# A two-layer fp32 model on one Trainium2 core: from generators advanced on an account to list scheduling of noted instructions

## The chip, the core and the metric

The kernel runs on one core of one Trainium2 chip. The metric is the device time of one execution in microseconds; lower is better. PE is the matrix engine (TensorE), PEld its weight loads, DVE the vector engine, ACT the scalar engine, POOL the GpSimd engine, SP the engine that issues the DMAs.

## What is computed

A sequence of 256 tokens (T = 256) with model width 1024 goes through two blocks of two layers each, in fp32. Every layer is a half-weighted SwiGLU feed-forward, a mixer, and a second SwiGLU feed-forward. The mixer of the first block joins a gated delta rule with stick-breaking attention; that of the second block uses three softmax attentions. Cut to what matters here:

```python
def swiglu(h, w_in, w_out):
    gate, up = jnp.split(h @ w_in, 2, axis=-1)
    return (jax.nn.silu(gate) * up) @ w_out

def hybrid_mixer(h, w_in, conv_w, a_log, dt_bias, ...):      # block 1
    dn_qkv, dn_z, dn_b, dn_a, sb_q, sb_k, sb_v, gate_a, gate_b = split_cols(h @ w_in)
    qkv = jax.nn.silu(causal_depthwise_conv(dn_qkv, conv_w))
    ...
    o_a = gated_delta_rule_chunked(q, k, v, g, beta)         # chunks of 64, a triangular solve in each
    y_a = (rmsnorm(o_a, dn_out_norm) * jax.nn.silu(dn_z)) @ w_branch_a
    y_b = stick_breaking_attention(rmsnorm(sb_q), rmsnorm(sb_k), sb_v) @ w_branch_b
    return (jax.nn.sigmoid(gate_a) * y_a + jax.nn.sigmoid(gate_b) * y_b) @ w_out
```

## The kernel before

**Dense products.** Activations lie feature-major in SBUF as `xh` and `xl`, two fp32r tiles whose sum is the fp32 value. A weight matrix is read in raw tiles of 128x1024 (four buffers, queue of SP), and each half of one, a piece of 128x512, is turned into `hi` (an fp32r copy, on ACT or by a CAST on DVE) and `lo` (a subtraction on DVE), up to seven pieces ahead of their use, in nine buffers. A product is then three matmuls per 128x128 block of weights: hi with xh, hi with xl, lo with xh. The program calls the psum tiles of these products `dn` (four of the eight banks) and those of all other work `acc` (four, shared).

**Stages.** The order is feed-forward, mixer, feed-forward, four times. The feed-forwards are dense products with little else. A mixer of block 1 (`mix1`, L736) runs, for the head pairs p = 0 to 3, the dense products dq, dk, dv, z(p-1), sq, sk, sv and ga(p), then z(3), gb(0) to gb(3), yb(0) to yb(3) (weights `w_branch_b`), and at last ya(0) to ya(3) (`w_branch_a`) and the output. Beside them stand four jobs `delta` (the delta rule of a head pair, L941: some 25 short groups of matmuls with a copy or a vector operation behind each: d_N, d_U, d_T, d_P, d_Ns, d_dec) and four jobs `stick` (L1148: b_qk, b_z, b_ss, b_tm). A mixer of block 2 (`mix2`, L1206) has softmax jobs in that place.

**What sets the order.** Every instruction is issued the moment the program reaches it, and `Clock.account` (L285) adds it to an account of the four engines. The jobs are Python generators in three queues a, b, c. Behind each k of a dense product `between` (L638) runs one short leftover (`pending`: taps of the convolution, squares) and `tick` (L497), which advances a queue by one step if the account says that the step's inputs are there and a psum bank is free:

```python
    def tick(self):
        for q in self.bg.values():
            if q and max(self.due.get(id(q), 0.0), self.nc.bank_free("acc", 4)) <= self.nc.free["tensor"]:
                self.step(q)

    def need(self, name, steps=1000):
        while self.done[name] < steps:
            self.step(min((q for q in self.bg.values() if q), key=lambda q: self.due.get(id(q), 0.0)))
```

At five places of `mix1` the program can't go on without a job: `need(("delta", p - 3))` (L804), `need(("stick", p - 1), 3)` (L822, ahead of sq(p)), `need(("delta", 1))` (L838), `need(("stick", 3))` (L845, ahead of yb) and `drain()` (L853, ahead of ya). There all steps that are left stand in a row, with no dense matmul between them.

**Choice of engine.** `split` and `copy` (L534, L547) take ACT unless the account lets DVE end it over 0.3 or 0.4 us earlier; `add` takes DVE or POOL. `acts` loads ACT's function table when the set of functions changes; a Copy needs no set of its own. In the rows of the profile nearly all instructions carry L226, the line of the helper that issues them, so they are told apart by their tiles.

Of the kernel before, what the change touches and what calls it, by code (L numbers as in the profile page):

```python
# [21 lines left out]
CP_A = 0.4  # L22
HI_A = 0.3
# [188 lines left out]

class Engine:


    def __init__(self, clock, name, eng):
        self.clock, self.name, self.eng = clock, name, eng

    def __getattr__(self, op):
        f = getattr(self.eng, op)  # L220

        def call(*args, **kw):
            aps = [a for a in list(args) + list(kw.values()) if isinstance(a, bass.AP)]
            if aps:
                self.clock.account(self.name, op, aps, kw)
            return f(*args, **kw)  # L226

        return call


class Clock:
    def __init__(self, nc):
        self.nc = nc
        self.free = {"tensor": 0.0, "vector": 0.0, "scalar": 0.0, "gpsimd": 0.0}
        self.ready = {}
        self.used = {}
        self.avail = {}
        self.slots = {}
        self.last = self.port = 0.0
        for n in self.free:  # L240
            setattr(self, n, Engine(self, n, getattr(nc, n)))
        self.sync = nc.sync

    def slot(self, pool, tag, bufs, tile_):

        h = self.slots.setdefault((pool, tag), [])
        if len(h) >= bufs:
            self.avail[tile_.tensor.name] = self.used.get(h.pop(-bufs), 0.0)
        h.append(tile_.tensor.name)
        return tile_  # L250

    def bank_free(self, tag, bufs):
        h = self.slots.get(("psum", tag), [])
        return self.used.get(h[-bufs], 0.0) if len(h) >= bufs else 0.0

    def cost(self, eng, op, out, ins):
        n = 1
        for d in (ins[0] if op == "tensor_reduce" else out).shape[1:]:
            n *= d
        psum = any(a.tensor.name.startswith(("dn_", "acc")) for a in [out] + ins)  # L260
        ptrs = sum(1 for a in ins[1:] if len(a.shape) == 2 and a.shape[1] == 1)
        if eng == "tensor":
            one = ins[0].dtype == R or op == "transpose"
            return max(n / 2.4e3, 0.107) + 0.002 if one else max(n / 0.6e3, 4 * ins[0].shape[-1] / 2.4e3) + 0.003
        if eng == "vector":
            two = not psum and op in ("tensor_copy", "tensor_scalar", "memset")
            return 0.07 + 0.06 * ptrs + n * (0.52e-3 if two else 1.04e-3) * (8 if op == "reciprocal" else 1)
        if eng == "scalar":
            return (0.055 if psum else 0.095) + n * 0.83e-3 + 0.093 * (len(ins) - 1)
        return 0.1 + n * {"tensor_scalar": 4e-3, "tensor_copy": 3.4e-3, "memset": 0.9e-3}.get(op, 2.2e-3)  # L270

    def shared(self, eng, out, ins):

        return eng == "gpsimd" or eng == "vector" and not any(
            a.tensor.name.startswith(("dn_", "acc")) for a in [out] + ins)

    def begins(self, eng, out, ins):
        at = max([self.free[eng], self.avail.get(out.tensor.name, 0.0)] + [self.ready.get(a.tensor.name, 0.0) for a in ins])
        return max(at, self.port) if self.shared(eng, out, ins) else at

    def ends(self, eng, op, out, ins):

        return self.begins(eng, out, ins) + self.cost(eng, op, out, ins)

    def account(self, eng, op, aps, kw):  # L285
        out, ins = aps[0], aps[1:]
        end = self.ends(eng, op, out, ins)
        self.free[eng] = end
        if self.shared(eng, out, ins):
            self.port = end  # L290
        for a in aps:
            self.used[a.tensor.name] = end + 0.1
        self.ready[out.tensor.name] = end + (0.07 if eng == "tensor" else 0.13)
        if eng != "tensor":
            self.last = max(self.last, end + 0.13)


class Stream:
# [43 lines left out]
    def split(self, upto):  # L342
        while self.nsplit < min(upto, len(self.pieces)):
# [6 lines left out]
            self.net.split(self.hi[u], self.lo[u], self.raw[r][:, o:o + n])  # L350
# [9 lines left out]
class Chunk:  # L360
    def __init__(self, stream, i):
        self.stream, self.i = stream, i
        self.kt, self.n = stream.shapes[i]

    def __call__(self, k, c, n):
# [8 lines left out]
        st.split(u + 1 + PIECE_AHEAD)  # L374
# [16 lines left out]
class Net:  # L391
    def __init__(self, ctx, tc, x, wsrc, small, out, parts):
        self.tc = tc
        self.nc = nc = Clock(tc.nc)
# [9 lines left out]
        self.act_set = None  # L404
        self.small_src, self.cmat_src = small
        self.bg = {"a": [], "b": [], "c": []}
        self.done = {}
        self.pending = []
        self.due = {}
# [3 lines left out]
    def t(self, shape, tag, bufs=1, dt=F, pool=None):  # L413
        self.uid += 1
        pool = pool or self.tp or self.cp
        return self.nc.slot(pool.name, tag, bufs, pool.tile(shape, dt, tag=tag, name=f"{tag}_{self.uid}", bufs=bufs))
# [7 lines left out]
    def scope(self, name):  # L424
        self.uid += 1
        old = self.tp
        with self.tc.tile_pool(name=f"{name}{self.uid}", bufs=1) as self.tp:
            yield
        self.tp = old

    def ps(self, shape, tag, bufs):
        self.uid += 1
        return self.nc.slot("psum", tag, bufs, self.pp.tile(shape, F, tag=tag, name=f"{tag}_{self.uid}", bufs=bufs))

    def bank(self, shape):
        return self.ps(list(shape), "acc", 4)

    def dn(self, shape=(128, 2, 256)):
        return self.ps(list(shape), "dn", 4)

    def acts(self, name):
        if self.act_set != name:
            self.nc.scalar.preload_act_table_set(name)
            self.nc.free["scalar"] += 1.3
            self.act_set = name
# [33 lines left out]
    def work(self, queue, name, gen):  # L479
        self.done[name] = 0  # L480
        q = self.bg[queue]
        if not q:
            self.due[id(q)] = self.nc.free["scalar"] + 0.15
        q.append((name, gen))

    def step(self, q):

        nc = self.nc
        nc.last = 0.0
        name, gen = q[0]  # L490
        self.done[name] += 1
        if next(gen, self) is self:
            q.pop(0)
            self.done[name] = 1000
        self.due[id(q)] = nc.last

    def tick(self):  # L497

        for q in self.bg.values():
            if q and max(self.due.get(id(q), 0.0), self.nc.bank_free("acc", 4)) <= self.nc.free["tensor"]:  # L500
                self.step(q)

    def need(self, name, steps=1000):

        while self.done[name] < steps:
            self.step(min((q for q in self.bg.values() if q), key=lambda q: self.due.get(id(q), 0.0)))

    def drain(self):
        for q in list(self.bg.values()):
            for name, _ in list(q):  # L510
                self.need(name)

# [3 lines left out]
    def load_x(self):  # L516
# [15 lines left out]
        self.x_sqs()  # L532

    def split(self, hi, lo, x, gain=None):  # L534

        nc = self.nc
        if gain is None:
            if nc.ends("scalar", "activation", hi, [x]) <= nc.ends("vector", "tensor_copy", hi, [x]) + HI_A:
                nc.scalar.activation(hi, x, AF.Copy)
            else:  # L540
                nc.vector.tensor_copy(hi, x)
            nc.vector.tensor_sub(lo, x, hi.bitcast(F))
# [4 lines left out]
    def copy(self, out, x, scale=None):  # L547

        nc = self.nc
        ins = [x] if scale is None else [x, scale]  # L550
        op = "tensor_copy" if scale is None else "tensor_scalar"
        if nc.ends("scalar", "activation", out, ins) <= nc.ends("vector", op, out, ins) + CP_A:
            if scale is None:
                nc.scalar.activation(out, x, AF.Copy)
            else:
                nc.scalar.activation(out, x, AF.Copy, scale=scale)
        elif scale is None:
            nc.vector.tensor_copy(out, x)
        else:
            nc.vector.tensor_scalar(out, x, scale, None, op0=OP.mult)  # L560
# [10 lines left out]
    def x_sqs(self):  # L571
        self.pending += [lambda b=b: self.x_sq(b) for b in range(4)]
# [10 lines left out]
    def add(self, out, a, b):  # L583

        nc = self.nc
        first = min(("vector", "gpsimd"), key=lambda e: nc.ends(e, "tensor_add", out, [a, b]))
        getattr(nc, first).tensor_add(out, a, b)
# [30 lines left out]
    def mm3(self, ps, w, x, js, start, stop):  # L618

        mm = self.nc.tensor.matmul  # L620
        for p, (a, b) in enumerate(((0, 0), (0, 1), (1, 0))):
            for j in js:
                mm(ps(j), w[j][a], x[b], start=(start(j) and p == 0), stop=(stop and p == 2), skip_group_check=True)
# [14 lines left out]
    def between(self, k, mid):  # L638
        if self.pending:
            self.pending.pop(0)()  # L640
        if mid and k == mid[0]:
            mid[1]()
        self.tick()

    def flush(self):
        while self.pending:
            self.pending.pop(0)()

    def dense_tok(self, key, xs, mid=None):
# [8 lines left out]
        for k in range(ch.kt):  # L658
            w = ch(k, 0, ch.n)
            for p, (a, b) in enumerate(((0, 0), (1, 0), (0, 1))):  # L660
                for i in range(2):
                    nc.tensor.matmul(ps[i], xs[a][k][:, i * 128:(i + 1) * 128], w[b],
                                     start=(k == 0 and p == 0 and (i == 0 or ch.n > 256)),
                                     stop=(k == ch.kt - 1 and p == 2), skip_group_check=True)
# [6 lines left out]
    def ffn(self, part, nxt):  # L671
# [4 lines left out]
        def out(c):  # L676
# [13 lines left out]
            final = nxt[1] == "final"  # L690
            for b in range(4):
# [12 lines left out]
            if not final:  # L704
                self.x_lo(3, g)
                self.x_sqs()

        for c in range(11):
# [880 lines left out]
```

## Time and profile before

| | us |
|---|---|
| time, median of 3 runs | 2794.15 (2793.99 to 2794.7) |
| profiled execution, its own time | 2791.08 |
| span of that execution | 2789.3 |
| PE busy | 2687.7 |
| DVE busy | 2051.2 |
| ACT busy | 1438.2 |

The profiled execution is 1.78 us longer than its span, and 3.07 us shorter than the median. The stages can be told in the trace by their tiles: the mixers of block 1 lie at 194.17 to 584.47 us and 951.31 to 1340.92 us, those of block 2 at 1708.03 to 1968.84 us and 2335.60 to 2594.08 us, the feed-forwards around them. The page has 40 slices with PE's busy share and the granted clock; the views by windows, by waits, and in order of time show each stage apart.

### The profile page before, as it was taken

What the parts mean: (1) busy time and instruction counts of PE and PEld (TensorE: products, weight loads), DVE (VectorE), ACT (ScalarE), POOL (GpSimd) and SP (SyncE); (2) the same over time, 40 slices, a digit from 0 to 9 for tenths busy, and PEclk for the clock granted to TensorE, in tenths of its full rate; (3) what the DMA queues carried; (4) which work ended last, traced back from release to release, by engine and by line L of the source; (5) the groups of instructions that cost most, each with busy time, mean ns of one, the idle gap of its engine ahead of it and who ended that gap; (6) DMA issues with size and microseconds to landing.
All of it is one profiled execution on the core that took longest, in us unless ns stands there. A gap on an engine that the chain in (4) does not pass through costs nothing.

```text
span 2789.3 us, 57423 instructions
## 1 busy us (share of the span) xinstructions
PE 2687.7 (96%) x22692; PEld 2644.8 (95%) x22692; DVE 2051.2 (74%) x4163; ACT 1438.2 (52%) x2870; POOL 75.7 (3%) x106
## 2 busy tenths in 40 slices
PE   8999799899999997998999999999999999999998
PEld 8999798899999997988999999989999999989998
DVE  7668878676676788886767767767767767767766
ACT  5456556454454575554545445545545445545543
POOL 0000001100000001010000000000000000000000
PEclk9999899999999998999999999999999999999999
DMA  6554334355555542333555554435555554445553
GB/s 232 189 177 158 122 103 148 103 186 192 195 189 190 171 170 99 111 135 118 191 195 193 196 196 148 151 135 174 193 195 175 197 196 146 157 131 182 191 188 129
DMA packets 128142, 463.45 MB, mean 166 GB/s; under 512 B 14336, under 2 KB 14592, under 8 KB 127744
## 3 DMA queue, kind: packets, MB, share of 16 engines
q1 hardware_dynamic: 127872, 459.78, 48.9%
q8 instruction: 178, 2.92, 0.4%
q14 instruction: 92, 0.75, 0.1%
HBM read 458.67 MB, written 1.05 MB: 165 GB/s over the span
## 4 chain that ended last, share of the span: by engine, by line
PE 86%; DVE 8%; ACT 3%; issue 2%; DMA 1%; DVEq 0%; SPq 0%; POOL 0%; ACTq 0%
PE dn L226 62%; PE acc L226 24%; DVE lo L226 3%; DMA raw<-in_w_dram 1%; ACT hi L226 1%; DVE d_prod L226 0%; DVE d_rows L226 0%; DVE dq L226 0%; ACT b_tm L226 0%; DVE d_dec L226 0%; DVE dk L226 0%; DVE d_Ub L226 0%; DVE pad L226 0%; DVE b_qk L226 0%; DVE d_Nb L226 0%
## 5 line engine op out<-in xcount | busy, mean ns | idle before, releaser
L226 DVE TENSOR_TENSOR lo<-raw,hi 128x512 fp32r<-128x512 f32 x1752 | 1148.9, 692 | 225.7 <-ACT hi L226 208.0
L226 ACT ACTIVATE hi<-raw 128x512 fp32r<-128x512 f32 (+1 forms) x1639 | 933.6, 617 | 265.6 <-PE dn L226 165.2
L226 PE MATMUL dn<-xh,hi 128*128 128x256 f32 x4208 | 842.6, 281 | 6.2 <-DVE hi L226 6.0
L226 PE MATMUL dn<-xl,hi 128*128 128x256 f32 x4208 | 828.2, 278 | 4.1 <-DVE xl L226 4.1
L226 PE MATMUL dn<-xh,lo 128*128 128x256 f32 x4208 | 826.7, 278 | 0.0
L226 PEld LDWEIGHTS dn<-xh,hi 128*128 128x128 f32 x4208 | 640.4, 189 | 16.3 <-issue 9.1
L226 PEld LDWEIGHTS dn<-xl,hi 128*128 128x128 f32 x4208 | 639.6, 189 | 5.8 <-DVE xl L226 5.6
L226 PEld LDWEIGHTS dn<-xh,lo 128*128 128x128 f32 x4208 | 639.2, 189 | 0.0
L226 PE MATMUL acc<-al,hi 128*128 128x256 f32 x1408 | 204.3, 282 | 0.0
L226 PE MATMUL acc<-ah,hi 128*128 128x256 f32 x1408 | 202.8, 281 | 0.0
L226 PE MATMUL acc<-ah,lo 128*128 128x256 f32 x1408 | 202.8, 281 | 0.0
L226 ACT ACTIVATE ah<-us 128x512 fp32r<-128x512 f32 x88 | 55.6, 632 | 283.4 <-DVE us L226 283.4
L226 PEld LDWEIGHTS acc<-ah,lo 128*128 128x128 f32 x1408 | 183.0, 189 | 0.0
L226 PEld LDWEIGHTS acc<-al,hi 128*128 128x128 f32 x1408 | 183.0, 189 | 0.0
L226 PEld LDWEIGHTS acc<-ah,hi 128*128 128x128 f32 x1408 | 181.6, 188 | 0.0
L226 ACT ACTIVATE gs<-gs 128x512 f32<-128x512 f32 x88 | 55.8, 635 | 228.3 <-DVE gs L226 228.3
L226 DVE TENSOR_TENSOR gs<-dn,nr 128x512 f32<-128x512 f32 x88 | 60.8, 691 | 104.3 <-PE dn L226 104.0
L226 DVE TENSOR_TENSOR us<-dn,nr 128x512 f32<-128x512 f32 x88 | 60.7, 690 | 102.2 <-PE dn L226 102.2
L226 PE MATMUL dn<-hi,xh 128*128 128x256 f32 (+2 forms) x640 | 134.7, 292 | 0.9 <-ACT v L226 0.9
L226 PE MATMUL dn<-lo,xh 128*128 128x256 f32 (+2 forms) x640 | 129.7, 284 | 0.0
L226 PE MATMUL dn<-hi,xl 128*128 128x256 f32 (+2 forms) x640 | 129.3, 283 | 0.0
L226 DVE TENSOR_TENSOR al<-us,ah 128x512 fp32r<-128x512 f32 x88 | 60.9, 692 | 61.4 <-ACT ah L226 61.4
(313 smaller groups left out, 2880.5 us busy)
## 6 DMA issues: line engine op xcount, KB each, us to landing
raw<-in_w_dram SPq DMA_DIRECT2D x853, 512.0 KB, 4.5
raw<-in_w_dram SPq DMA_DIRECT2D x14, 384.0 KB, 3.8
raw<-in_w_dram SPq DMA_DIRECT2D x4, 408.0 KB, 4.1
cmat<-in_cmat_dram SPq DMA_DIRECT2D x1, 1216.0 KB, 9.3
x<-in_x_dram SPq DMA_DIRECT2D x4, 256.0 KB, 5.4
out_dram<-x SPq DMA_DIRECT2D x4, 256.0 KB, 2.6
cmat<-in_cmat_dram SPq DMA_DIRECT2D x1, 648.0 KB, 8.0
raw<-in_w_dram SPq DMA_DIRECT2D x2, 272.0 KB, 3.1
```

What stands on the lines that cost most here:

```text
L226: return f(*args, **kw)
```

## The change

Nothing is issued any more when the program reaches it. `Sched.note` (L286 of the new program) records an instruction with its operands, works out from the regions that they cover which earlier ones it depends on, and puts it on a list. At the end of each scope (`heads` and `merge` of mix1, a feed-forward, the end) `flush` (L338) emits the whole list on the account of the engines: it takes the engine that can start something earliest, and on it the ready instruction of the lowest `rank`. On PE anything that is not a dense matmul goes first and the dense matmuls keep their order; on ACT and DVE it goes by the time of readiness, and the `hi` or `lo` of a weight piece by the time of its use less 5.0 or 4.0 us. Calls to `need`, `drain`, `tick`, `pending` and the `yield`s are gone. The core of the diff:

```diff
+    SLACK = {"vector": 4.0, "scalar": 5.0}
...
+    def rank(self, e, s, at, t):
+        if t.stream:
+            return (1, 0.0, t.seq)
+        if e in ("tensor", "sync"):
+            return (0, at if e == "tensor" else 0.0, t.seq)
+        key = at
+        if t.piece is not None:
+            n = self.use.get(t.piece, self.nstream + 12 * (t.piece - self.last))
+            key = max(s, self.free["tensor"]) + (n - self.done_stream) * 0.1135 - self.SLACK.get(e, 4.0)
+        if e == "scalar" and t.table is not None and t.table != self.table:
+            key += 2.0
+        return (0, key, t.seq)
```

```diff
+        for eng, (op, args, kw) in alts.items():
...
+            func = args[2] if eng == "scalar" and op == "activation" else None
+        t.table = self.want if "scalar" in alts and func not in (AF.Copy, AF.Square) else None
...
+        if e == "scalar" and t.table is not None and t.table != self.table:
+            self.nc.scalar.preload_act_table_set(t.table)
```

```diff
-        if nc.ends("scalar", "activation", out, ins) <= nc.ends("vector", op, out, ins) + CP_A:
...
+            self.nc.note({"scalar": ("activation", (out, x, AF.Copy), {}), "vector": ("tensor_copy", (out, x), {})})
...
-        st.split(u + 1 + PIECE_AHEAD)
+        st.split(min(u + 1 + PIECE_AHEAD, PIECE_BUFS + (u if self.held is None else self.held)))
```

Three more things change with it. The psum banks get fixed lanes: in mix1 two for each parity of `delta`, one for `stick` and three for the dense products (four before). `add` takes DVE alone. A copy or a `hi` that may run on either engine is noted with ACT's form first and DVE's second, and since `func` is taken from the last form, it carries the table that is wanted at that place of the program. Over the whole program the table loads go from 49 to 178 (in each mix1 from 13 to 63); DVE has 4050 instructions instead of 4013 (a few CASTs less, more copies), ACT 2624 ACTIVATEs instead of 2661; PE's matmuls, POOL's and SP's instructions keep their numbers. PE enters work other than dense products some 385 times in each mix1, instead of 260.

Two places. PE in the first mix1, before: the end of the dense product z(1) (`hi`, `lo` with `xh`, `xl` into dn_4352), the rows of delta and stick that follow, and the first of sq(2) (dn_4562):

```order
L226 MATMUL dn_4352<-hi_4268,xl_14_85 128x256 x2
L226 MATMUL dn_4352<-lo_4269,xh_9_80 128x256 x2
L226 MATMUL acc_4444<-b_z_3633,sbv_3172 128x256
L226 MATMUL acc_4444<-b_z_3633,sbv_3172 128x128
L226 MATMUL acc_4451<-d_T_814_4387,d_Ns_708_3878 128x128 x4
L226 MATMUL acc_4481<-d_U_786_4219,d_P_826_4456 128x128 x4
L226 MATMUL acc_4523<-d_T_814_4387,d_N_597_3285 32x32 x8
L226 MATMUL acc_4534<-d_U_786_4219,d_P_837_4488 32x32 x8
L226 MATMUL acc_4550<-ident,sbraw_3723 128x128 x4
L226 MATMUL acc_4556<-ident,sbraw_3816 128x128 x4
L226 MATMUL dn_4562<-hi_4290,xh_6_77 128x256 x2
```

Now the first of these, b_z with sbv, stands in the midst of another dense product (into bank_71):

```order
L419 MATMUL bank_71<-hi_114,xl_12_89 128x256 x2
L419 MATMUL bank_71<-lo_115,xh_7_84 128x256 x2
L419 MATMUL bank_71<-hi_114,xh_7_84 128x256
L419 MATMUL bank_70<-b_z_2273,sbv_2269 128x256
L419 MATMUL bank_70<-b_z_2273,sbv_2269 128x128
L419 MATMUL bank_70<-b_z_2273,sbv_2269 128x256
L419 MATMUL bank_70<-b_z_2273,sbv_2269 128x128
L419 MATMUL bank_71<-hi_114,xh_7_84 128x256
```

What stood in one row between two dense products stands in several pieces between dense matmuls; the same holds for the rows of the last delta, whose final transposes (ident, d_dec) were the last ahead of ya and now have 31 matmuls of yb(3) behind them.

ACT in the first mix1, before: the sigmoids of the gates mb (tiles dq, dk, dv, pad) at the start of yb, and the pieces behind them:

```order
L226 ACT_TABLE_LOAD
L226 ACTIVATE dq_6057<-dq_6057 128x512
L226 ACTIVATE dk_6058<-dk_6058 128x512
L226 ACTIVATE dv_6059<-dv_6059 128x512
L226 ACTIVATE pad_6060<-pad_6060 128x2x256
L226 ACTIVATE hi_6618<-raw_6306 128x512
L226 ACTIVATE hi_6634<-raw_6306 128x512
```

Now, at the same sigmoids:

```order
L413 ACT_TABLE_LOAD
L419 ACTIVATE d_P1_76_2229<-bank2_68 128x512
L413 ACT_TABLE_LOAD
L419 ACTIVATE hi_19_97<-raw_18_96 128x512
L413 ACT_TABLE_LOAD
L419 ACTIVATE dv_124_2277<-dv_124_2277 128x512
L413 ACT_TABLE_LOAD
L419 ACTIVATE d_P1_76_2229<-bank2_68 32x4x32
L413 ACT_TABLE_LOAD
L419 ACTIVATE hi_34_114<-raw_17_95 128x512
```

The four sigmoids were under one load; now copies and pieces stand between them, each with a load ahead of it.

## Rows read from the trace of the kernel before

**Rows 1.** Page, section 1: busy time, share of span, instructions.

```profile
PE 2687.7 (96%) x22692; PEld 2644.8 (95%) x22692; DVE 2051.2 (74%) x4163; ACT 1438.2 (52%) x2870; POOL 75.7 (3%) x106
```

**Rows 2.** Windows by stage: mix1, mix1, mix2, mix2, feed-forwards; busy time, granted clock.

```profile
core 0: us, PE busy (x) PEld busy (x) DVE busy (x) ACT busy (x) POOL busy (x), PEclk, DMA share, GB/s
194.17:584.47 390.30, 355.54 (x2967) 347.48 (x2966) 317.66 (x870) 221.18 (x500) 31.65 (x48) 0.94 0.39 131
951.31:1340.92 389.61, 355.03 (x2966) 347.15 (x2965) 317.74 (x870) 221.09 (x500) 31.87 (x48) 0.95 0.38 131
1708.03:1968.84 260.81, 253.54 (x2036) 241.58 (x2034) 196.31 (x373) 135.50 (x298) 3.91 (x1) 0.98 0.44 148
2335.60:2594.08 258.48, 252.74 (x2036) 240.60 (x2034) 196.18 (x373) 135.54 (x298) 3.91 (x1) 0.99 0.46 150
584.47:951.31 366.84, 366.19 (x3174) 365.89 (x3173) 253.12 (x415) 179.60 (x317) 0.00 (x0) 1.00 0.56 190
```

**Rows 3.** Windows of the first mix1's five half-clock stretches, and their sum.

```profile
475.20:492.30 17.10, 13.52 (x78) 11.45 (x79) 12.87 (x53) 4.41 (x8) 2.21 (x2) 0.50 0.04 15
...
sum 44.47, PE 30.70 PEld 27.62 DVE 35.03 ACT 19.15 POOL 3.59; mean PE 6.14 PEld 5.52 DVE 7.01 ACT 3.83 POOL 0.72
```

**Rows 4.** The same sum for the second mix1, six half-clock stretches.

```profile
sum 41.20, PE 28.73 PEld 26.51 DVE 33.07 ACT 17.39 POOL 3.36; mean PE 4.79 PEld 4.42 DVE 5.51 ACT 2.90 POOL 0.56
```

**Rows 5.** The same sum for both mix2, three half-clock stretches.

```profile
sum 17.10, PE 15.05 PEld 14.54 DVE 16.51 ACT 6.03 POOL 0.00; mean PE 5.02 PEld 4.85 DVE 5.50 ACT 2.01 POOL 0.00
```

**Rows 6.** Waits of PE: releaser, us in total, times, longest.

```profile
PE acc L226 <- ACT b_z L226: 23.8, 4, 9.4
PE acc L226 <- DVE d_dec L226: 9.0, 2, 4.5
PE acc L226 <- DVE b_ss L226: 8.0, 2, 4.0
...
PE dn L226 <- DVE lo L226: 6.6, 2, 3.3
PE dn L226 <- DVE hi L226: 6.0, 1, 6.0
PE dn L226 <- issue: 4.9, 1, 4.9
```

**Rows 7.** Timeline of PE: start, duration, tiles, idle before and releaser; end of z(1).

```profile
317.36 0.39 PE L226 MATMUL dn<-lo,xh 128*128 128x256 f32 x2
327.19 2.93 PE L226 MATMUL acc<-b_z,sbv 128*128 128x256 f32 x8 [9.44 <-ACT b_z L226]
...
341.64 0.69 PE L226 MATMUL dn<-hi,xh 128*128 128x256 f32 x2
```

**Rows 8.** Timeline of PE at dv(0): last dense matmul, then the decay's.

```profile
215.21 0.39 PE L226 MATMUL dn<-xh,lo 128*128 128x256 f32 x2
220.52 1.44 PE L226 MATMUL dn<-g_g,cmat 128*128 128x16 f32 x6 [4.92 <-issue]
```

**Rows 9.** Windows ahead of and in the bunch behind z(1).

```profile
240.00:310.00 70.00, 70.00 (x602) 69.79 (x601) 61.08 (x168) 47.69 (x114) 3.18 (x4) 1.00 0.50 167
...
320.00:330.00 10.00, 2.81 (x9) 2.45 (x10) 9.85 (x16) 5.51 (x9) 2.68 (x2) 0.58 0.33 105
```

**Rows 10.** Groups of ACT by form: busy, mean ns, idle before.

```profile
L226 ACT ACTIVATE hi<-raw 128x512 fp32r<-128x512 f32 x1595 | 914.5, 621 | 242.3 <-PE dn L226 162.0 <-DMA raw<-in_w_dram 42.6 <-PE acc L226 21.6
L226 ACT ACT_TABLE_LOAD x49 | 62.9, 1283 | 1.6 <-PEq L1585 0.7
```

**Rows 11.** Timeline of ACT around a table load.

```profile
327.05 0.61 ACT L226 ACTIVATE hi<-raw 128x512 fp32r<-128x512 f32 x1
327.68 1.28 ACT L226 ACT_TABLE_LOAD   x1
328.97 0.63 ACT L226 ACTIVATE dk<-dk 128x512 f32<-128x512 f32 x1
329.51 0.61 ACT L226 ACTIVATE dq<-dq 128x512 f32<-128x512 f32 x1
```

More of the change, by code (lines that the diff above doesn't have):

```diff
@@ L1 @@
+import heapq
 import math
@@ L210, with __init__ @@
 CWIDTH = [sum(v.shape[1] for v in d.values()) for d in CONSTS]
+class Task:
+    __slots__ = ("run", "cost", "outs", "ins", "preds", "succs", "at", "end", "piece", "table", "stream", "port", "seq", "on")
 class Engine:
-    def __init__(self, clock, name, eng):
-        self.clock, self.name, self.eng = clock, name, eng
+    def __init__(self, sched, name, eng):
+        self.sched, self.name, self.eng = sched, name, eng
     def __getattr__(self, op):
-        f = getattr(self.eng, op)
         def call(*args, **kw):
[L223 to L226, printed above, removed]
-        return call
@@ L256, in cost, with psum @@
-    def cost(self, eng, op, out, ins):
+        self.todo, self.seq = [], 0
+        self.acc = {}
+        self.port = self.dma = 0.0
+        self.table = None
+        self.tail, self.use, self.last = None, {}, 0
+        self.nstream = self.done_stream = 0
+        self.want = None
+    def psum(self, aps):
+        return any(a.tensor.name.startswith("bank") for a in aps)
+    def cost(self, eng, op, out, ins, nacc):
         n = 1
@@ L259, in cost @@
             n *= d
[L260 removed]
+        psum = self.psum([out] + ins)
         ptrs = sum(1 for a in ins[1:] if len(a.shape) == 2 and a.shape[1] == 1)
         if eng == "tensor":
[L263 to L264 removed]
+            if ins[0].dtype == R:
+                return n / 2.4e3 + 0.0075
+            return max(n / 2.4e3, 0.107) + 0.002 if op == "transpose" else \
+                max(n / 0.6e3, 4 * ins[0].shape[-1] / 2.4e3) + 0.003
@@ L270, in cost @@
+        if eng == "sync":
+            return 0.06
         return 0.1 + n * {"tensor_scalar": 4e-3, "tensor_copy": 3.4e-3, "memset": 0.9e-3}.get(op, 2.2e-3)
[L272 to L279, printed above, removed]
@@ new lines, in emit @@
+    def emit(self, t, e, s):
+        f, args, kw = t.run[e]
+        if e == "scalar" and t.table is not None and t.table != self.table:
+            self.nc.scalar.preload_act_table_set(t.table)
+            self.table = t.table
+            s += 1.3
+        if e == "gpsimd" or e == "vector" and t.port:
+            s = max(s, self.port)
+            self.port = s + t.cost[e]
+        f(*args, **kw)
+        t.on, t.at, t.end = e, s, s + t.cost[e]
+        self.free[e] = t.end
+        if e == "sync":
+            out = args[0]
+            size = 4
+            for d in out.shape:
+                size *= d
+            self.dma = max(self.dma, s) + size / 250e3
+            t.end = max(self.dma, s) + 2.0
+        if t.stream:
+            self.done_stream += 1
@@ L428, in scope, with bank @@
             yield
+            self.nc.flush()
         self.tp = old
[L431 to L436, printed above, removed]
+    def bank(self, shape, lane="acc"):
+        own = self.lanes[lane]
+        own.append(own.pop(0))
+        return self.view(self.banks[own[-1]], list(shape))
     def dn(self, shape=(128, 2, 256)):
-        return self.ps(list(shape), "dn", 4)
+        return self.bank(shape, "dn")
     def acts(self, name):
[L442 to L445, printed above, removed]
+        self.nc.want = name
     def consts(self):
@@ L477, in sm @@
         return self.small[:, a:b]
[L479 to L511, printed above, removed]
     def gain(self, p):
@@ L837, in mix1 @@
             self.acts(SET_SILU)
-            self.need(("delta", 1))
             self.zs[3] = self.z_silu(zps)
+            next(late.pop(), None)
             mb = [t([128, 2, T], kind, 3, pool=keep) for kind in ("dq", "dk", "dv")]
@@ L1488, in run @@
             self.sq_tag = lambda b, mix1=p[:2] == (1, "mix"): (f"d_P{b % 2}", 1) if mix1 else ("sq", 4)
+            self.lanes = {k: list(v) for k, v in LANES[p[1] == "mix" and p[0]].items()}
             if p[1] == "mix":
```

331 lines of the change are left out of this document (183 added, 148 removed).

## The prediction

> **What bounds the kernel now.** I read the page's busy times first: PE is busy for 2687.7 of 2789.3 us, DVE for 74%, ACT for 52% [rows 1]. PE is the bound, so the question is where it isn't at work, or is at work slowly. The windows by stage answer it [rows 2]. A pair of feed-forwards of 366.84 us leaves PE idle for 0.65 us, at full clock: nothing is to be had there. The first mix1 lasts 390.30 us with PE busy for 355.54, so 34.76 idle; the second 389.61 − 355.03 = 34.58. The two mix2 leave 7.27 and 5.74.
>
> Idle time isn't all. The granted clock is at half, 1.2 instead of 2.4 GHz, in some stretches of each mixer that follow an idle time of PE; in the first mix1 they hold 30.70 us of busy PE [rows 3], in the second 28.73 [rows 4], in both mix2 together 15.05 [rows 5]. At full clock that work takes half as long, so 15.35, 14.37 and 7.5 us go to the clock. What a mixer could give back:
> - first mix1 34.76 + 15.35 = 50.1 us
> - second mix1 34.58 + 14.37 = 49.0 us
> - both mix2 7.27 + 5.74 + 7.5 = 20.5 us
>
> Together 119.6 us. The floor of this kernel with PE's work as it is would be 2791.08 − 119.6 = 2671.5 us.
>
> Then the waits of PE [rows 6]: at the top stand results of delta and stick (b_z 23.8 us in four waits, d_dec 9.0 in two, b_ss 8.0 in two), no weight piece. The timeline shows the place [rows 7]: the last matmul of z(1) starts at 317.36, the first of sq(2) at 341.64, and the 24.3 us between hold only short groups of the jobs, with a wait of 9.44 for b_z at their head. These are the rows that `need` puts in a line. Where jobs and dense matmuls alternate there is no such loss: 240 to 310 us is seven full windows, PE busy for 70.00 of 70.00 [rows 9]. So it isn't the jobs' work that costs, but that their chains run alone.
>
> **The change part by part.** *The forced rows go.* In the new order the rows behind z(1) stand in pieces between dense matmuls, and so do those ahead of yb and ya. If nothing new waits, PE has both the idle and the clock back: −50.1 and −49.0. Idle and clock fall together, since the clock in rows 3 and 4 only drops behind idle time.
>
> *What is late next in mix1.* Of the full length, 390.30 − 50.1 = 340.2 us, I subtract three residues in each mixer.
> (a) dv(0): the decay's matmul comes 4.92 us after PE had nothing else [rows 8], and the clock is low behind it. The norm's matmul moves ahead, but it is a chain of small steps on three engines; I leave 2 us (0 to 8).
> (b) ACT. The loads go up by 50 in each mix1. One load lasts 1.283 us [rows 10]; an ACTIVATE behind another starts 0.54 us later, behind a load 1.92 (from 327.05 to 328.97), so a load costs 1.38 [rows 11] and 50 cost 69 us. ACT's 221.18 us [rows 2] become 290 in 340: not the bound on the average, but in gb and yb, where copies, pieces and sigmoids alternate with loads, some 20 of these stand close together, 28 us. Nine buffers of pieces cover some of this. I leave 4 us (0 to 15).
> (c) DVE. It is busy for 61.08 of the 70 us in which PE runs without a gap, and for 9.85 of 10 behind z(1) [rows 9]: in that place it is DVE's backlog that PE waits for, and the new order has the same work and a few copies more. Over all of mix1 its 317.66 us fit in 340.2, so the backlog can be spread, if only with little to spare. I leave 3.5 us (0 to 12).
> Sum 9.5 us (0 to 35), so −40.6 and −39.5, together −80.
>
> *mix2.* Its waits are those for `lo` (3.3 us each) [rows 6] and for jobs at the ends of its parts. The pieces are held there by buffers, which the change keeps, so the list can't do much for those. Half of 20.5: −10 (0 to −20.5).
>
> *The start.* PE waits 6.0 us for the first `hi`, which DVE makes [rows 6]. Now ACT makes it, behind small xh instructions, a square and one more load of 1.283 us: +1.5 (0 to +3).
>
> *Feed-forwards.* The other 29 loads, 29 × 1.38 = 40 us, lie beside an ACT that is idle for 187 of 366.84 us [rows 2], and the pieces are made ahead. If that cover fails, a load ahead of a silu that a product waits for would show. 0 (0 to +3). `add` on DVE alone, and the lanes of psum (three banks for dense products in mix1), have no row that prices them: a dense product uses one bank or two, so a third is free while one is evacuated; 0, within the bounds of (c).
>
> Sum: 2791.08 − 80 − 10 + 1.5 = 2702.6 for the profiled execution. The median lies 3.07 above it: 2705.7, **2706 us**.
>
> A rule of the Trainium skill speaks against the change. "ScalarE: Activation LUTs", section "What ACT_TABLE_LOAD costs", gives a switch of sets 1283 ns for the load and some 1380 ns for a drain, 2.66 us in all. The rows agree with the first (1283) and not with the second, since dk starts 0.01 us after the load's end [rows 11]. By the page 50 switches would be 133 us, ACT would need 354 us in mix1 and be its bound, and the sum would be 2791.08 − 2 × 36 − 10 + 1.5 + 3.07, about 2714; I go by the rows.
>
> **The rivals.**
> *Half comes back.* The wait moves instead of going: PE's forced rows are gone, but dense matmuls then wait for pieces that DVE and ACT make late, because the two are filled in bursts (DVE at 9.85 of 10, ACT with 20 loads in gb and yb). For it: (b) and (c) above, and that an engine that runs its instructions in order waits for each one that comes later than the account holds. Against it: 70 us without a gap at 87% DVE. With half of 119.6 given back: 2791.08 − 59.8 + 1.5 + 3.07 = 2736.
>
> *In-order groups.* PE now enters the jobs' work some 385 times in each mix1, at the moment of the account and ahead of any dense matmul; each entry that comes before its input is there holds the dense matmuls behind it. Every 0.1 us on the mean of 770 entries costs 77 us; at 0.155 us each all 119.6 are gone and the time is 2794, and the clock would fall in addition only if the waits are long. Against it: no wait in the stretch of rows 9, which has such entries. With 0.08 us each it is 2794 − 119.6 + 62, about 2736 again, so the two share a case and differ in what the waits name.
>
> *Slower: the table loads on the path.* The price is 129 × 1.38 = 178 us, the place gb and yb, where the last delta's copies out of psum (d_P) each have a load ahead of them, and dense products behind them. A load that a d_P copy or a late piece waits for is on PE's path. If two thirds of it are (119.6 / 178 = 0.67), nothing is left of the gain; if all are, 2791.08 − 119.6 + 178 + 3 = 2852. For it: ACT's order now. Against it: with the loads in it ACT is still idle for some 50 us of each mix1 (340 − 290), and only a wait that PE can't fill with dense matmuls counts. The rule "Batch activation calls by set", same page of the Trainium skill, section "Table sets: the hidden batching unit", speaks for this case.
>
> *It doesn't do what it says.* The list is only as good as the account's estimates. Were those of the jobs' chains too short by as much as the forced rows cost, PE would wait for the same results at other places: no change, 2794.
>
> **How the numbers follow.** Chances: the forecast (2675 to 2722) 0.58; half comes back, by bursts or by early groups (2722 to 2760) 0.25; most is lost again but not all (2760 to 2788) 0.07; no change 0.04; slower 0.06. The bounds of the parts give 2791.08 − 119.6 + 3.07 = 2674.5 below, and 2791.08 − 29.1 + 3 + 3 + 3.07 = 2771 above (residues of 35 in each mix1, nothing in mix2). For 8 in 10 I take 2680 to 2752, which leaves out the last few us above the floor and the upper part of the worse cases. A measurement of this kernel tells 0.2%, 5.6 us, from no change: faster 0.90, same 0.04, slower 0.06.
>
> **What would show it.** In the profile after: each mix1 at about 350 us with PE's idle time under 10 and a granted clock near 1.00; no stretch like the 24.3 us behind z(1); b_z, d_dec and b_ss gone from the top of PE's waits. (b) would show as PE waiting for ACT `hi` or d_P at gb and yb, (c) as PE waiting for DVE `lo` in dq(3) to z(2), (a) as an idle time at dv(0). The table loads should number 178 at 1.28 us. It would be wrong by in-order groups if PE's wait list held hundreds of short waits for acc tiles (now by their bank's name), and by half if the windows of mix1 kept 20 us or more of idle time, or the clock stayed at 0.95. A feed-forward pair that isn't 366.8 us would mean that I missed something outside the mixers.

## The result and the profile after

The changed kernel takes 2720.61 us (median of 4 runs, 2718.03 to 2721.76) against 2794.07 us for the kernel before on the same chip: a ratio of 0.9736, 95% interval 0.9719 to 0.9753. The forecast was 2706 us with a range of 2680 to 2752. The profiled execution took 2721.43 us, its span 2719.7. The page's totals and, by stage, windows over the two mix1, the two mix2 and a pair of feed-forwards (length, busy time of each engine, granted clock, DMA share):

```profile
PE 2690.2 (99%) x22692; PEld 2623.5 (96%) x22692; DVE 2021.5 (74%) x4200; ACT 1648.0 (61%) x2962; POOL 72.3 (3%) x106
```

```profile
core 0: us, PE busy (x) PEld busy (x) DVE busy (x) ACT busy (x) POOL busy (x), PEclk, DMA share, GB/s
197.37:545.63 348.26, 347.86 (x2966) 338.42 (x2965) 305.23 (x895) 277.16 (x526) 30.02 (x48) 1.00 0.44 150
913.06:1260.93 347.87, 347.42 (x2966) 337.60 (x2965) 305.21 (x895) 276.82 (x526) 30.60 (x48) 1.00 0.44 150
1628.36:1892.07 263.71, 261.56 (x2035) 239.43 (x2034) 199.00 (x377) 141.70 (x293) 3.62 (x1) 0.99 0.45 150
2259.46:2523.28 263.82, 261.10 (x2036) 238.80 (x2034) 198.65 (x377) 141.41 (x293) 3.62 (x1) 0.99 0.48 150
545.63:913.06 367.43, 366.61 (x3174) 366.33 (x3173) 250.45 (x409) 200.15 (x330) 0.00 (x0) 1.00 0.56 186
```

Beside rows 2: each mix1 is 42 us shorter (390.30 and 389.61 before), PE's idle time in it is 0.4 us instead of 34.7, and the clock is at 1.00. But each mix2 is longer (260.81 and 258.48 before), although its idle time fell from 7.27 and 5.74 to 2.15 and 2.72. The span is 69.6 us shorter: the mix1 give 83.8, the mix2 take 8.2, the start 3.1, the feed-forwards 2.8.

The waits of PE in the whole kernel, beside rows 6 (releaser, us in total, times, longest):

```profile
PE bank L419 <- ACT hi L419: 9.8, 2, 9.1
PE bank L419 <- DVE k L419: 3.2, 4, 1.4
PE bank L419 <- DVE gs L419: 3.1, 4, 0.8
PE bank L419 <- DVE lo L419: 1.4, 1, 1.4
PE bank L419 <- DVE dqk L419: 1.2, 4, 0.3
PE bank L419 <- ACT d_P L419: 0.6, 2, 0.3
PE bank L419 <- DVE s_s L419: 0.4, 2, 0.2
```

b_z, d_dec and b_ss are gone, and 9.1 of the 9.8 us for `hi` are the start. So PE hardly waits for anything, and still mix2 grew. Where did that go? Into PE's own busy time. Set against PE's work before at full clock, 340.2 us in the first mix1, it is now 347.86, that is 7.7 more; the second mix1 has 6.8 more by the same sum (rows 2, 4), both mix2 together 522.7 instead of 506.3 − 7.5 = 498.8, 23.9 more (rows 2, 5). The matmuls are the same; PE's busy time for them grew by 38.3 us. A small part of this is still the clock: each mix2 keeps one stretch of 3.42 us, from 1679.88 and from 2311.34 us, in which PE is busy throughout at a granted clock of 0.50, behind idle time of PE. Half of the two stretches is 3.4 us, so some 34.9 us are matmuls that take longer. Of the 119.6 us in idle and clock nearly all came back, all but 5.7 us of idle time, and these 38.3 went the other way: −119.6 + 5.7 + 38.3 = −75.6, and the four mixers measured −75.5.

The place can be seen in the first mix2. Two stretches of PE's timeline (start, duration, tiles, number of records), first after:

```profile
1769.66 0.43 PE L419 MATMUL bank<-s_pT,vt 128*64 128x128 f32 x2
1770.02 0.49 PE L419 MATMUL bank<-dqk 64*128 64x128 f32 x2
1770.43 0.65 PE L419 MATMUL bank<-s_pT,vt 128*64 128x256 f32 x2
1771.01 0.70 PE L419 MATMUL bank<-dqk 64*128 64x256 f32 x2
1771.63 0.43 PE L419 MATMUL bank<-s_pT,vt 128*64 128x128 f32 x2
1772.00 0.33 PE L419 MATMUL bank<-ident,s_s 128*128 128x128 f32 x1
```

and before, a dqk row of two heads with the dense matmuls around it, and one of a single head:

```profile
1868.90 0.39 PE L226 MATMUL dn<-xh,lo 128*128 128x256 f32 x2
1869.22 0.93 PE L226 MATMUL acc<-dqk 64*128 64x128 f32 x8
1870.08 0.50 PE L226 MATMUL dn<-xh,hi 128*128 128x256 f32 x2
...
1874.07 0.92 PE L226 MATMUL acc<-dqk 64*128 64x128 f32 x4
```

Two softmax jobs alternate matmul by matmul: 10 records from 1769.66 to 1772.00, 0.234 us each. Before, a job's row stood whole: 8 dqk records from 1869.22 to 1870.08, 0.108 each. (The scores of a head are two matmuls, and each leaves two records.) The 4 records of a single head last 0.92 us, as long as the 8 of two heads (0.93). A dqk matmul uses 64 of PE's rows, and in the row of 8 one of the other head runs beside it, on the other 64. In the mixed stretch none does. This stretch is part of a longer one: from 1767.87 to 1779.38 us, 11.5 us, there is no dense matmul. Short matmuls go first in the new order, so here the softmax jobs bunch up; before, no two dense matmuls of a mix2 started more than 3.6 us apart. In mix1 it is the other way round, at most 2.6 us instead of 24.2. The Trainium skill ("TensorE: Matmul & The Clock Gate", section "The mechanism" of "Packing small matmuls") says of tiles in different row groups that they overlap in the array. The row of 8 agrees.

### The profile page after: what moved, and what is told of

It is laid out like the page before. It is cut to its first block, busy times and chain, and to the rows that moved or that the text cites. A ratio compares the mean times of both kernels' runs of the same rounds, so it can differ in the third digit from the quotient of the medians.

```text
span 2719.7 us, 57647 instructions
## 1 busy us (share of the span) xinstructions
PE 2690.2 (99%) x22692; PEld 2623.5 (96%) x22692; DVE 2021.5 (74%) x4200; ACT 1648.0 (61%) x2962; POOL 72.3 (3%) x106
## 4 chain that ended last, share of the span: by engine, by line
PE 94%; DVE 3%; ACT 3%; issue 1%; DMA 0%; DVEq 0%; SPq 0%; ACTq 0%
PE bank L419 94%; ACT L413 1%; DVE lo L419 1%; ACT hi L419 0%; DVE nvs L419 0%; DVE dqk L419 0%; DVE s_mx L419 0%; ACT b_tm L419 0%; DVE k L419 0%; DVE nr L419 0%; DVE hi L419 0%; DMA x<-in_x_dram 0%; DVE s_s L419 0%; DVE gs L419 0%; ACT dk L419 0%
## 5 line engine op out<-in xcount | busy, mean ns | idle before, releaser
L419 PE MATMUL bank<-xh,hi 128*128 128x256 f32 x4208 | 833.4, 278 | 13.4 <-ACT hi L419 9.8
L419 PE MATMUL bank<-xh,lo 128*128 128x256 f32 x4208 | 834.2, 278 | 1.4 <-DVE lo L419 1.4
L419 PE MATMUL bank<-xl,hi 128*128 128x256 f32 x4208 | 832.0, 278 | 0.0
L419 PEld LDWEIGHTS bank<-xh,hi 128*128 128x128 f32 x4208 | 639.2, 188 | 15.6 <-ACT hi L419 14.6
L419 PEld LDWEIGHTS bank<-xh,lo 128*128 128x128 f32 x4208 | 639.4, 188 | 3.3 <-DVE lo L419 1.7
L419 PEld LDWEIGHTS bank<-xl,hi 128*128 128x128 f32 x4208 | 638.5, 188 | 3.3 <-issue 3.0
L419 PE MATMUL bank<-al,hi 128*128 128x256 f32 x1408 | 204.1, 282 | 0.0
L419 PE MATMUL bank<-ah,lo 128*128 128x256 f32 x1408 | 203.0, 281 | 0.0
L419 PE MATMUL bank<-ah,hi 128*128 128x256 f32 x1408 | 202.9, 281 | 0.0
L419 PEld LDWEIGHTS bank<-ah,lo 128*128 128x128 f32 x1408 | 183.2, 189 | 0.0
```

## Experiments

### Rows of short matmuls kept whole

The changed kernel, and matmuls outside the dense products that are noted one right after another are emitted together. `run[t]` is that row, and a row is ready when all its operands are:

```diff
+            run[b] = run[a] if not solo and a in run and "tensor" in a.run and not a.stream and a.seq + 1 == b.seq else []
+            run[b].append(b)
...
-            self.emit(t, e, s)
+            for m in run[t]:
+                self.emit(m, e, max(s, self.free[e]))
```

> The changed kernel (2720.6 us), but matmuls outside the dense products that are noted one right after another are emitted as one row on PE, once all of them are ready. Theory A (PE's own short matmuls got dearer: in the first mix2 the same 278 records cost 53.7 us between dense matmuls instead of 37.0, in mix1 71 where some 64 are possible, because rows that used to stand together are split and mixed with those of another job): about 2720.6 - 2 x 16 - 2 x 6 = 2677 us, each mix2 near 248 us, each mix1 near 342. Theory B (ACT's 129 added table loads and DVE's backlog keep PE from the full gain): within 5 us of 2720, or slower, since groups start later.

Measured: 2690.06 us, ratio to the kernel before 0.9625 (0.9612 to 0.9638). Windows over the same four mixers:

```profile
198.39:542.22 343.83, 342.07 (x2967) 335.63 (x2965) 304.79 (x888) 279.56 (x531) 32.83 (x48) 1.00 0.46 152
909.64:1253.29 343.65, 342.34 (x2966) 336.22 (x2965) 304.60 (x888) 279.29 (x531) 32.86 (x48) 1.00 0.46 152
1620.71:1871.39 250.68, 248.13 (x2035) 237.00 (x2034) 197.52 (x378) 140.48 (x292) 3.60 (x1) 1.00 0.50 158
2238.69:2491.45 252.76, 250.25 (x2035) 238.74 (x2034) 197.73 (x378) 140.64 (x292) 3.60 (x1) 0.99 0.51 157
```

PE's busy time falls by 5.8, 5.1, 13.4 and 10.9 us, 35.2 of the 38.3, of which 1.7 is one half-clock stretch less (the first mix2 is at 1.00). The four mixers are 32.7 us shorter, the kernel 30.6. In the timeline the same two jobs now stand one behind the other:

```profile
1754.97 2.16 PE L428 MATMUL bank<-s_pT,vt 128*64 128x256 f32 x12
1757.06 3.43 PE L428 MATMUL bank<-dqk 64*128 64x128 f32 x24
1760.42 0.50 PE L428 MATMUL bank<-xh,lo 128*128 128x256 f32 x2
```

That is 0.174 us for a record of s_pT and 0.140 for one of dqk, where the mixed stretch had 0.234. Its six records of s_pT and four of dqk would take 1.6 us at these rates, or 1.9 with the 0.84 us that the four of a single head took before, instead of 2.34. Theory A holds, with 30.6 us where 44 were expected.

### Ready matmuls by their place in the program

```diff
-            return (0, at if e == "tensor" else 0.0, t.seq)
+            return (0, 0.0, t.seq)
```

> The changed kernel, with ready short matmuls on PE taken by their place in the program instead of by the time they became ready: 434 changes of operands on PE instead of 626 (346 with whole rows, 360 in the kernel before). Theory A: the time follows the changes, so about 2720.6 - 30.6 x (626 - 434) / (626 - 346) = 2700 us, most of the gain in mix2. If only an unbroken row helps: within 5 us of 2720.

Measured: 2697.31 us, ratio 0.9653 (0.9638 to 0.9667). A change of operands is a place in PE's order where a short matmul has other operands than the short one ahead of it. Between the changed kernel (626 changes of operands outside the dense products, 2720.6 us) and the run with whole rows (346 changes, 2690.1), 434 changes should give 2700. By this estimate each change of operands on PE costs about 30.6 / 280 = 0.11 us here.

### Two heads' scores one after the other

The kernel before, with the loops over parts and heads exchanged in mix2's scores:

```diff
-        for part in range(2):
-            for ps, (_, q, k, _) in zip(banks, heads):
+        for ps, (_, q, k, _) in zip(banks, heads):
+            for part in range(2):
```

> The kernel before, with one edit: the scores of two heads in mix2 are computed head after head instead of part after part, so that two matmuls on different halves of PE's rows no longer follow one another. Nothing else moves. Theory A says such neighbours run together (pitch 0.007 us between two mqk records, 0.109 for dqk, where one alone takes 0.109 or 0.216): about 9 pairs in each mix2 cost 0.35 us more each, 3 us per mix2, 6 in all: 2800 us. If the order of neighbours on PE does not matter: 2794, the mix2 windows unchanged.

Measured: 2796.29 us, ratio 1.0005 (0.9996 to 1.0014), no change. A row of dqk:

```profile
1873.40 0.93 PE L226 MATMUL acc<-dqk 64*128 64x128 f32 x8
1874.26 0.50 PE L226 MATMUL dn<-xh,hi 128*128 128x256 f32 x2
```

It takes 0.86 us from its start to the next dense matmul, as before. In the trace the records of the two heads still start in pairs, 0.014 us apart (0.007 before), although one head's are now all issued ahead of the other's. So this part of the theory fell: the order of the two heads within their row doesn't matter. What costs is another job in between, or a row broken into pieces.

### The same order, without the loads of plain copies

An account with all loads sets the order, and a load is issued only where a function other than Copy or Square needs another table; the order of all instructions is that of the changed kernel.

```diff
-            self.nc.scalar.preload_act_table_set(t.table)
             self.table = t.table
...
+        if e == "scalar" and t.needs and t.table != self.loaded:
+            self.nc.scalar.preload_act_table_set(t.table)
+            self.loaded = t.table
```

> The changed kernel with every instruction of every engine in the same order, and 84 table loads instead of 178: the account still counts the loads that a plain Copy seemed to need, but they are not issued. It is the clean form of the earlier run with fewer loads, whose 6 us more in each mix1 came with another order on PE. Theory A (PE's own short matmuls, loads beside them): mix1 347 to 348 us and mix2 263 to 264 as in the changed kernel; the start and the feed-forwards behind a mixer 1.3 us less each, some 5 places, so 2714 us. Theory B (loads on PE's path): 94 x 1.38 = 130 us of ACT less, mix1 shorter by 4 us or more each, 2705 or below. If the longer mix1 of the earlier run came from the missing loads themselves: mix1 354, 2725.

Measured: 2717.41 us, ratio 0.9727 (0.9713 to 0.9742); the interval overlaps that of the changed kernel. The first mixer and the loads that are left:

```profile
198.54:546.35 347.81, 346.61 (x2967) 337.64 (x2966) 304.62 (x895) 236.61 (x495) 28.59 (x48) 1.00 0.46 150
```

```profile
L421 ACT ACT_TABLE_LOAD x83 | 106.5, 1283 | 1.4
```

ACT is busy 40.6 us less in that mixer, and its length is 347.81 instead of 348.26. The second mix1 lasts 347.89 us instead of 347.87. So in mix1 the 94 added loads that this run leaves out lie beside PE's work, and Theory B, which wanted 4 us or more there, falls. At the start the first matmul comes 1.4 us earlier, but mix1 begins 1.2 us later, with a half-clock stretch of 3.41 us ahead of it. The two mix2 are 1.6 and 2.7 us shorter (262.12 and 261.15 us); the half-clock stretch that each has in the changed kernel is missing here, which is 3.4 us. Whether the loads bring these stretches on isn't shown.

### No table for a plain copy, in the account too

```diff
-            func = args[2] if eng == "scalar" and op == "activation" else None
+            if eng == "scalar":
+                func = args[2] if op == "activation" else None
```

> The changed kernel, but a copy or a weight piece that may run on either engine carries no function table when ACT's form is a plain Copy: 80 table loads instead of 178. Theory A (loads lie beside PE's work): only the second load ahead of the first piece counts, 1.3 us, so about 2719 us and the mixers as they are (mix1 348, mix2 264). Theory B (loads hold up the copies that PE waits for): 100 loads x 1.38 us = 138 us of ACT less, of which a tenth or more shows: 2707 or below.

Measured: 2727.41 us, ratio 0.976 (0.9746 to 0.9773), slower than with the loads, which neither theory had (the two intervals overlap at their ends). Windows over both mix1:

```profile
194.22:548.74 354.52, 351.94 (x2966) 338.75 (x2965) 297.90 (x871) 247.71 (x516) 33.46 (x48) 1.00 0.45 147
915.83:1270.49 354.66, 352.29 (x2966) 339.09 (x2965) 297.90 (x871) 247.85 (x516) 32.95 (x48) 1.00 0.45 147
```

They are 6 to 7 us longer, with PE's busy time up by 4.1 and 4.9: the account's other order has 646 changes of operands instead of 626. That the missing loads themselves cost nothing was shown by the run above; that all of the 6 us are changes of operands was not.

### First load and first piece early

The first table load is issued at the start of the program, and the first piece is split on DVE:

```diff
+        nc.nc.scalar.preload_act_table_set(SET_EXP)
...
+        if piece == 0:
+            nc.note({"vector": ("tensor_copy", (hi, x), {})}, piece)
```

> The changed kernel, but the first table load is issued at the very start and the first weight piece is split on DVE, as in the kernel before. The first matmul came at 9.12 us instead of 6.00 because a load (1.28 us) waits behind x, then a square (0.5) and a second load (1.28) stand ahead of the piece. If that is all of it: first matmul near 6.0 to 6.5 us and about 2718 us (2717.5 to 2719). If the later start is hidden by something else: 2720.6.

In the changed kernel, the chain at the start (start, duration, what):

```profile
4.41 1.28 ACT L419
5.70 0.91 ACT xh L419 x2
6.61 0.52 ACT sq L419
7.13 0.02 issue
7.15 1.28 ACT L413
...
8.44 0.64 ACT hi L419
...
9.12 2.93 PE bank L419 x12
```

Measured: 2716.66 us, ratio 0.972 (0.9707 to 0.9734), and the first matmul at 6.32 us:

```profile
6.32 0.76 PE L419 MATMUL bank<-xh,hi 128*128 128x256 f32 x2 [6.32 <-DVE hi L419]
```

The start has 2.8 of its 3.1 us back. The total is 4 us lower, a little more than expected, though by less than the intervals can tell.

### Weight pieces ahead of job steps

The changed kernel with one line changed:

```diff
-    SLACK = {"vector": 4.0, "scalar": 5.0}
+    SLACK = {"vector": 30.0, "scalar": 30.0}
```

> The changed kernel with one number changed: a weight piece counts as due 30 us ahead of its use (4 and 5 before), so that ACT and DVE take a free piece buffer before a job's step, and the steps wait. In the changed kernel the first stick is done 25 us after its first transposes, in the kernel before 75 us; if it is the priority of job steps over pieces that makes the jobs end early, this run gives that back: the last transposes of delta come behind the last of yb again (with a wait of PE ahead of ya, some 8 to 15 us in each mix1), mix1 356 to 365 and about 2720.6 + 2 x 12 = 2745. If the list alone does it, whatever goes first: within 5 us of 2720.

Measured: 2799.88 us, ratio 1.0018 (1.0009 to 1.0028): the whole gain is gone. Windows over both mix1, and two of PE's waits in the whole kernel:

```profile
198.13:571.64 373.51, 358.04 (x2966) 345.39 (x2965) 320.71 (x913) 278.11 (x514) 29.61 (x48) 0.97 0.43 140
945.35:1316.29 370.94, 354.89 (x2966) 342.24 (x2965) 320.47 (x913) 277.64 (x514) 29.66 (x48) 0.98 0.43 141
```

```profile
PE bank L419 <- DVE gs L419: 11.3, 3, 3.8
...
PE bank L419 <- DVE b_qk L419: 9.1, 2, 4.6
```

Idle time (15.5 and 16.1 us) and low clock are back in mix1, with a wait for stick's b_qk of up to 4.6 us, and both mix2 and three of the feed-forwards are some 6 us longer each, with waits for a feed-forward's own `gs`. So the list alone isn't the gain: without the rule that a piece waits while a job's step can run, nothing is left of it. That was three times as dear as I expected. Whether the old generators would gain as much by such a rule, without the list, wasn't tried.

### Fewer pieces ahead in the kernel before

```diff
-PIECE, PIECE_AHEAD, PIECE_BUFS = 512, 7, 9
+PIECE, PIECE_AHEAD, PIECE_BUFS = 512, 4, 9
```

> The kernel before with one number changed: weight pieces are made up to 4 ahead of their use instead of 7, generators and forced places as they were. It tells whether holding the pieces back is enough without the list. The order it gives has the first stick's end 210 dense matmuls earlier than before (2286 instead of 2496) and no forced row longer than 18 matmuls (30 to 38 before). If job steps behind pieces on ACT and DVE are what made the jobs late: mix1 some 370 us instead of 390 and about 2755 us in all. If fewer pieces ahead only make PE wait for pieces, or if it takes the list to order the steps: 2790 or more, with hi or lo among PE's waits.

Measured: 2806.19 us, ratio 1.0038 (1.0024 to 1.0053). Windows over a mix1 and a mix2, and the first of PE's waits:

```profile
195.24:576.80 381.56, 355.96 (x2967) 343.38 (x2965) 321.66 (x881) 213.69 (x488) 28.80 (x48) 0.98 0.41 133
...
1692.07:1968.91 276.84, 259.13 (x2035) 245.84 (x2034) 197.03 (x375) 135.27 (x294) 3.86 (x1) 0.96 0.44 140
```

```profile
PE dn L226 <- DVE lo L226: 44.6, 47, 3.3
PE dn L226 <- ACT hi L226: 32.1, 23, 2.5
```

The forced rows are shorter, the longest time between two dense matmuls in mix1 being 6.5 us instead of 24.2, and this mix1 is 8.7 us shorter. But now PE waits for pieces, 44.6 us for `lo` and 32.1 for `hi` (6.6 and 0.7 before), and mix2 is 16 us longer. Of the two fixed numbers tried, 7 makes the jobs late and 4 the pieces; 5 and 6 weren't tried. The change holds a piece by the time of its use and lets it pass when that nears, which neither number does.

### All three edits, and a hold

Whole rows, no table for a plain copy and the early start together; then, in addition, a row may interrupt dense matmuls only once it has been ready for 0.8 or 2.0 us on the account:

```diff
+            if e == "tensor" and self.in_stream and not t.stream and s - at < 0.8:
+                st = [x for x in a if x[2].stream]
+                if st:
+                    at, _, t = st[0]
```

> The changed kernel with three edits together: rows of short matmuls kept whole, no function table for a plain Copy, early first load and first piece on DVE. Theory A: they add up if the order on PE is then the same, 2690.1 - 4 for the start - 6 for the loads at stage ends = 2680 us, with mix1 near 342 and mix2 near 250. If the longer mix1 of the run with fewer loads comes from finer mixing on PE, it must be gone here, since rows are whole (350 changes of operands on PE instead of 646): mix1 at most 344. If it comes from elsewhere: mix1 350, 2692.

> As the three edits together, and a short row may interrupt the dense matmuls only once it has been ready for 0.8 us on the account; once PE is in such a row, all that are ready follow: 169 interruptions in the program instead of 211. If each interruption costs PE some 0.15 us by itself (dense to short 0.2 instead of 0.11, short to dense 0.31 instead of 0.22): 42 x 0.15 = 6 us less than the three edits, about 2674. If the 0.8 us make the chains of delta late: 2680 or more, with PE waits for acc tiles.

> As the three edits with a hold of 0.8 us (2677.7 us), but the hold is 2.0 us: 137 interruptions of the dense matmuls instead of 169. If an interruption costs PE 0.15 to 0.2 us and the chains have room: 32 x 0.17 = 5 us less, 2672. If the chains of the last delta or of mix2's softmax jobs have no room for it: 2678 or more, with the wait ahead of ya or at dqk.

> As the three edits with a hold of 0.8 us, but ordered on an account that still has the table loads that plain Copies seemed to need, which are then not issued. With loads in the account the run with whole rows had mix1 at 343.8 us, without them 346.2, though fewer loads can't cost time. If the account with loads happens to give the better order: 2 to 4 us less than 2677.7. If that difference was chance: 2675 to 2681.

| | us | ratio (95%) |
|---|---|---|
| three edits | 2689.95 | 0.9626 (0.9612 to 0.9641) |
| and a hold of 0.8 us | 2677.71 | 0.9582 (0.9566 to 0.9598) |
| and a hold of 2.0 us | 2676.87 | 0.9582 (0.9566 to 0.9598) |
| hold of 0.8 us, loads in the account only | 2686.54 | 0.9618 (0.9604 to 0.9632) |

The three edits don't add up: together they are no faster than whole rows alone. The hold gives 12 us more, twice the 6 that I had for it, and a longer one nothing beyond that; why it is twice stays open. An account with the loads in it orders worse, not better. These versions differ by the order alone, and up to 9 us lie between orders that I can't rank in advance. With a hold of 2.0 us the mixers are

```profile
195.51:536.77 341.26, 339.31 (x2966) 334.45 (x2965) 295.42 (x867) 246.86 (x518) 30.54 (x48) 1.00 0.47 153
904.45:1246.45 342.00, 339.30 (x2967) 334.46 (x2966) 295.40 (x867) 246.59 (x518) 30.52 (x48) 1.00 0.47 153
1613.78:1863.57 249.79, 246.54 (x2035) 238.67 (x2034) 196.38 (x376) 142.55 (x295) 3.64 (x1) 0.99 0.49 159
2230.65:2479.52 248.87, 246.11 (x2035) 238.26 (x2034) 196.19 (x376) 142.40 (x295) 3.64 (x1) 0.99 0.51 159
```

with PE's busy time at 339.3 in mix1, below the 340.2 of the kernel before at full clock: all that the changed kernel lost to mixing in mix1 is back. This version beats both kernels, by 4.2% and by some 44 us.

## Why the prediction was right, and where it was off

**What bounds it.** Right. The 119.6 us of idle time and low clock in the mixers were the thing to have, they came back nearly whole, and the clock came back with the idle time, but for one stretch of 3.42 us in each mix2.

**The total.** The parts below are 18.8 us off in sum (2702.6 forecast for the profiled execution, 2721.43 measured). The median came out 0.8 us below that execution and not 3.07 above it, so it is off by 14.9 only; that is luck.

**mix1.** Forecast −80, measured −83.8: right in size, but by another term. I subtracted 9.5 us in each for waits at dv(0), behind ACT and behind DVE. All PE's idle time there is 0.4 us, so these three residues are nought; instead PE's own matmuls cost 7.7 and 6.8 us more. The two happen to be alike, so this number is luck in part.

**ACT's loads.** I left them 4 us in each mix1 and gave 0.06 to the rival in which they make the kernel slower. The windows put ACT at 277 us in mix1, below my 290, and the run without 94 of them moved the mixer by 0.4 us. The rule of the Trainium skill ("ScalarE: Activation LUTs", section "What ACT_TABLE_LOAD costs") on 2.66 us for a switch did not show. By its figure the 50 added loads of a mix1 would be an estimated 133 us and would have put ACT above PE. In the chain at the start the next instruction of ACT begins 0.01 us behind each of the two loads (5.69 to 5.70, 8.43 to 8.44 us).

**mix2.** The step that failed. I forecast −10 (0 to −20.5) and it measured +8.2. The bound at 0 rested on idle time alone: I took PE's work in mix2 as given, and weighed only how much of the idle time the list could reach. The idle time did fall by 8.1 us in the two; 23.9 us more of PE's busy time than the work at full clock were not in the sum, 3.4 of them left-over clock and the rest dearer matmuls. The profile before had the row for it: 8 dqk records of two heads last as long as 4 of one, and the new order showed jobs alternating on PE. I had looked at that order for mix1 only, and counted interruptions of the dense matmuls, not changes among the short ones.

**The start.** Forecast +1.5 (0 to +3), measured +3.1: also the first load, which I had not moved, now waits behind x (1.28 us).

**Feed-forwards.** Forecast 0 (0 to +3), measured +2.8 in all, 0.1 to 0.6 us a stage and 1.2 in the last.

**The rivals.** Half came back: no, the waits did not move to pieces. In-order groups: PE is interrupted more often, though far less than I put it. Counted in the trace, a short matmul follows a dense one at 87 places in each mix1, 62 before; the 385 and 260 that I gave as entries count something else, so the prices per entry that I worked out from 770 don't hold. And the waits in its list sum to 20 us, the start among them; the price was not waiting but the matmuls themselves, which I had no rival for. No change: it did not come. But the run with pieces first has that time, 2799.88 us, by another cause, so the gain hangs on two numbers, 4.0 and 5.0 us.

## What to carry to other kernels

Where one in-order engine is fed by others that also prepare its weights, work ahead by the time of use rather than by a count: here the same list with early pieces gave back all it had won, and the count of 4 traded one wait for another. When a scheduler mixes jobs on PE, cost the matmuls in their new neighbourhood too, and keep rows of one shape whole; idle time that is filled can come back as longer busy time. A busy engine with slack, like ACT here, takes many small losses for nothing, and the profile's waits of the bound engine say so at once.

## What the runs showed of the hardware

I had not expected that short fp32 matmuls cost so much by their neighbours: 0.140 to 0.174 us for a record in whole rows of dqk or s_pT, 0.234 where the two alternate, and by the estimate above about 0.11 us for each change of operands over the whole kernel. The order of heads within one row made no difference (0.86 us for 8 records either way). And 94 table loads of 1.283 us, issued between copies that PE depends on, moved the kernel by 3 us, within what the runs can tell.
